# Two-layer decoder trunk: the first x transfers issued by ScalarE, the first weight tile brought in two parts

## The chip, the cores and the metric

One core of one Trainium2 chip runs the whole program. The metric is device microseconds of one execution; the median of three runs of the kernel before is 276.29 us (276.09 to 276.38).

## The reference, cut to what matters

Two layers, 256 tokens, model width 1024, everything in float32:

```python
for l in range(2):
    h = rms_norm(x, g_pre[l])
    qa, ka, va, ga, qb, kb, vb, gb, rb, qm, gm = split(h @ w_in[l])      # 1024 -> 3344
    oa = causal_attention(norm(qa), norm(ka), va) * silu(ga)             # 8 heads of 64, ALiBi
    ob = rms_norm(gated_linear_attention(qb, kb, vb, rb)) * silu(gb)     # 4 heads
    mk, mv = split(rms_norm(mem, g_mem[l]) @ w_mem_kv[l])
    om = attention(norm(qm), norm(mk), mv) * silu(gm)                    # 256 memory tokens
    x = x + concat(oa, ob, om) @ w_out[l]
```

With 256 tokens the block-sparse attention of the reference has one block, and so is plain causal attention.

## The kernel before, in words

**Products in three parts.** Every float32 operand of a large product is split into a high part, rounded to the format `fp32r`, and the low rest: `xh`, `xl` of x (times the gain `g_pre`), `whi`, `wlo` of a weight, `oh`, `ol` of the memory tokens and later of the attention outputs. A product is high by high, high by low and low by high, three TensorE matmuls (L1013 for one weight tile, L1020 for two tiles of one unit side by side). ScalarE writes a high part of a weight (L347 for the first tile, L406 for later ones) and VectorE the low part behind it (L349, L408). For x and the memory tokens the high part is ScalarE's (L260) or GpSimd's (L262) and the low part VectorE's (L302).

**The first unit.** The columns `vr` (272) and `kq` (256) of the first layer's input projection are one DRAM array `w0` of 8 tiles of 128 rows, one for each k; x lies beside it in 8 tiles k, the first with the parameters ahead of it (array `xp`). TensorE runs k = 0 to 7, at each k twelve matmuls: six of `vr` and six of `kq`. The table `LOADS` lists the transfers in the order in which `start_loads` issues them, as (x or w, first k, last k + 1, planned time of landing); all are on SyncE's queue. The reader `first_x` makes `xh` and `xl`, `first_w` makes `whi` and `wlo`, at k = 0 already in two pieces, and `first_sq` adds the squares of x for the norm (L310 on ScalarE, L315 and L318 on VectorE, called sqs). While the first data are on their way, `main` runs `WARM` matmuls on zeros (L1050).

**What sets the order.** The code is a planner: every step is a generator that asks for an engine with a cost and an earliest time, and the step that could begin first is written out next. So a change of one planned time (those of `LOADS`, `cst_ev`, the cost of the first step in `main`) moves steps on every engine, until the plans meet again. Each engine then runs its list in order. A transfer's completion is one of eight semaphores in turn, and a transfer that takes a semaphore over waits until the one before it on that semaphore has landed.

**What follows the first unit.** Weight tiles of 1 MB come through three buffers `raw`, one transfer each (L364); a tile's transfer waits for the last VectorE read of the tile before it in that buffer. The unit `ga0`, the pairs `va0 va1` and `qa0 ka0`, then the pair `mk mv` over the memory tokens follow on TensorE. The memory tokens (`memT`) are split into `oh`, `ol` and their squares summed by VectorE (L318 again); two short matmuls (L440) finish that sum. In the forget gate's chain ScalarE takes an absolute value, an exponential and, after a table load, a logarithm (L537 to L541), then VectorE makes `z` (L543) and the running sum `b` (L545).

Of the kernel before, what the change touches and what calls it, by code (L numbers as in the profile page):

```python
# [16 lines left out]
P = 128  # L17
# [11 lines left out]
PAIRK = 0  # L29
SPLIT = 7  # L30
MEMPRIO = 6
WARM = 6
FSQ = 7
STATS = 300
LOADS = (("x", 0, 1, 3100), ("w", 0, 1, 4300), ("x", 1, 2, 4600), ("w", 1, 2, 5300), ("x", 2, 4, 6000),
         ("w", 2, 3, 6700), ("w", 3, 4, 7600), ("x", 4, 6, 8300), ("w", 4, 6, 9900), ("x", 6, 8, 10600),
         ("w", 6, 8, 12100))
NB = 528
ENTER, LEAVE, CROSS = 89.0, 189.0, 60.0
SLACK, HOLD = 300.0, 900.0  # L40
# [128 lines left out]
def trunk(ctx, tc, xp_d, w0_d, memT_d, wvr_d, win_d, wmkv_d, wout_d, wup_d, cst_d, nb_d, out_d):  # L169
# [66 lines left out]
    def op(eng, cost, after=0.0, prio=None, table=None, mode="full"):  # L236
        return ("op", [(eng, cost)], after, prio, table, mode)
# [7 lines left out]
    def scost(n, psum=False, ptr=0):  # L245
        return (55 if psum else 95) + 0.83 * n + 93 * ptr
# [75 lines left out]
    def start_loads():  # L322
# [6 lines left out]
        for what, a, b, t in LOADS:  # L329
            if what == "x":  # L330
                xs = slice(L * NPRM + a * T if a else 0, L * NPRM + b * T)
                nc.sync.dma_start(xp[:, xs], xp_d[:, xs])
                plan.spawn(first_x(a, b, t), 30 - 2 * a)
            else:
                nc.sync.dma_start(raw[:, a:b], src[:, a:b])
                plan.spawn(first_w(a, b, t, raw, hi, lo, got), 29 - 2 * a)
        plan.spawn(first_sq(), 5)
        nc.sync.dma_start(cst, cst_d)
        cst_ev.set(12800)
        nc.sync.dma_start(wup, wup_d)  # L340

    def first_w(a, b, t, raw, hi, lo, got):
        for k in range(a, b):
            for n, cs in (("vr", slice(0, 272)), ("kq", slice(272, NB))) if k == 0 else (("vk", slice(0, NB)),):
                w = cs.stop - cs.start
                t1 = yield op("S", scost(w), t)
                S.activation(hi[:, k, cs], raw[:, k, cs], AF.Copy)  # L347
                t2 = yield op("V", vcost(w), t1)
                V.tensor_sub(lo[:, k, cs], raw[:, k, cs], hi[:, k, cs].bitcast(F32))  # L349
                for x in ("vr", "kq") if n == "vk" else (n,):  # L350
                    wts[0, x][k].set(t2)
        if b == KT:
            raws.release(got, t2)

# [690 lines left out]
            wrel[l, nm][k // 2].set(t)  # L1045

    def main():
        yield op("P", 4700, 0.0, None, None, "main")
        for j in range(WARM):
            TE.matmul(banks.slots[7][2][:, 0:256], lhsT=zero[:, 0:128], rhs=zero, start=True, stop=True)  # L1050
        idx = {(l, n): i for i, (l, n, _, _) in enumerate(seq)}
# [218 lines left out]
```

## Time and profile before

| what | value |
|---|---|
| median of three runs | 276.29 us (276.09 to 276.38) |
| the profiled execution's own time | 276.73 us |
| its span in the trace | 274.9 us |
| TensorE busy, matmuls | 269.3 us (98% of the span) |
| VectorE busy | 226.5 us (82%) |
| ScalarE busy | 195.2 us (71%) |
| GpSimd busy | 88.6 us (32%) |
| bytes moved | 45.76 MB, mean 166 GB/s |

The span is what the trace holds; 1.83 us of the profiled execution lie outside of it. Rows give start and duration in us. A matmul's shown duration overlaps the next one, so the pace of TensorE is read from start to start: 0.12 us for a matmul of 256 or 272 columns and 0.23 us for one of 512. Idle time in square brackets stands ahead of the row's instruction, with what ended it.

### The profile page before, as it was taken

The page shows a single profiled execution, that of the slowest core. Times are in us where ns is not written, and L with a number is a line of the kernel's source. Part 1 is how long each engine was busy: PE and PEld are TensorE (multiplying, and loading weights), DVE is VectorE, ACT ScalarE, POOL GpSimd, SP SyncE. Part 2 cuts the span into 40 slices and gives each one's busy share as a digit, 9 for nine tenths or more (in the row PEclk, how much of TensorE's full clock was granted, in tenths as well). Part 3 has the DMA queues.
Part 4 walks back from the last instruction along what each step waited for, and adds up shares of the span by engine and source line. Part 5 has one row for each costly group of instructions (what it writes and reads, how often), then busy time and mean ns, then how long its engine had stood idle before and what let it go on. Part 6 is the DMA issues. An engine that isn't in the chain of part 4 may idle for free.

```text
span 274.9 us, 5873 instructions
## 1 busy us (share of the span) xinstructions
PE 269.3 (98%) x2184; PEld 240.0 (87%) x2184; DVE 226.5 (82%) x573; ACT 195.2 (71%) x437; POOL 88.6 (32%) x107
## 2 busy tenths in 40 slices
PE   8999999999999999999999999999999999999994
PEld 7898887778998998999999887789888788999994
DVE  3998999989767998989897998989797787898621
ACT  5858995987986977957675796766986755975500
POOL 3312295650452551500062426322235520420000
PEclk9999999999999999999999999999999999999999
DMA  7999618460744142444465537048034325170111
GB/s 208 389 358 367 246 12 316 151 286 10 299 155 153 20 182 110 154 164 153 162 242 175 204 139 294 13 139 321 4 153 150 159 91 218 20 273 14 57 60 38
DMA packets 8556, 45.76 MB, mean 166 GB/s; under 512 B 960, under 2 KB 2384, under 8 KB 3536
## 3 DMA queue, kind: packets, MB, share of 16 engines
q1 hardware_dynamic: 8528, 45.39, 44.9%
q8 instruction: 17, 0.28, 0.4%
q14 instruction: 11, 0.09, 0.1%
HBM read 44.34 MB, written 1.05 MB: 165 GB/s over the span
## 4 chain that ended last, share of the span: by engine, by line
PE 86%; DVE 5%; DMA 4%; issue 1%; POOL 1%; SPq 1%; ACT 1%; POOLq 0%; DVEq 0%
PE bank L1013 48%; PE bank L1020 21%; PE bank L962 4%; PE bank L947 3%; PE bank L895 3%; DMA raw<-memT_dram 2%; PE bank L504 2%; DMA xp<-xp_dram 2%; DVE wlo L408 1%; POOL oh L262 1%; PE bank L747 1%; DVE sqs L318 1%; DVE ol L302 1%; PE bank L623 1%; PE bank L702 0%
## 5 line engine op out<-in xcount | busy, mean ns | idle before, releaser
L408 DVE TENSOR_TENSOR wlo<-raw,whi 128x512 fp32r<-128x512 f32 (+1 forms) x144 | 97.4, 699 | 13.5 <-ACT whi L406 12.1
L406 ACT ACTIVATE whi<-raw 128x512 fp32r<-128x512 f32 (+1 forms) x144 | 86.4, 625 | 20.8 <-PE bank L1013 8.9
L1013 PE MATMUL bank<-xh,whi 128*128 128x256 f32 x160 | 46.3, 289 | 0.0
L1013 PE MATMUL bank<-xl,whi 128*128 128x256 f32 x160 | 44.5, 278 | 0.0
L1013 PE MATMUL bank<-xh,wlo 128*128 128x256 f32 x160 | 44.5, 278 | 0.0
L932 POOL TENSOR_SCALAR pe<-pe,rc 128x256 f32<-128x256 f32 (+1 forms) x48 | 27.3, 583 | 39.9 <-DVE rc L929 27.0
L1013 PE MATMUL bank<-oh,whi 128*128 128x256 f32 x128 | 35.9, 280 | 0.0
L1013 PE MATMUL bank<-ol,whi 128*128 128x256 f32 x128 | 35.8, 280 | 0.0
L1013 PE MATMUL bank<-oh,wlo 128*128 128x256 f32 x128 | 35.7, 279 | 0.0
L484 POOL TENSOR_TENSOR cc<-ss,nhalf 128x8 f32<-128x8 f32 x12 | 20.9, 1746 | 42.0 <-DVE ss L482 35.2
L1020 PE MATMUL bank<-whi,xh 128*128 128x512 f32 x80 | 32.7, 409 | 0.0
L1013 PEld LDWEIGHTS bank<-xh,whi 128*128 128x128 f32 x160 | 30.1, 188 | 1.6 <-issue 1.4
L1020 PE MATMUL bank<-wlo,xh 128*128 128x512 f32 x80 | 31.4, 393 | 0.0
L1020 PE MATMUL bank<-whi,xl 128*128 128x512 f32 x80 | 31.3, 391 | 0.0
L1013 PEld LDWEIGHTS bank<-xl,whi 128*128 128x128 f32 x160 | 30.1, 188 | 0.1
L1013 PEld LDWEIGHTS bank<-xh,wlo 128*128 128x128 f32 x160 | 30.2, 189 | 0.0
L1013 PE MATMUL bank<-whi,xh 128*128 128x256 f32 (+1 forms) x96 | 28.1, 293 | 0.0
L1013 PE MATMUL bank<-wlo,xh 128*128 128x256 f32 (+1 forms) x96 | 27.6, 287 | 0.4 <-DVE wlo L349 0.3
L1013 PE MATMUL bank<-whi,xl 128*128 128x256 f32 (+1 forms) x96 | 27.1, 282 | 0.0
L1013 PEld LDWEIGHTS bank<-oh,wlo 128*128 128x128 f32 x128 | 24.3, 190 | 0.0
L1013 PEld LDWEIGHTS bank<-oh,whi 128*128 128x128 f32 x128 | 24.0, 188 | 0.2 <-issue 0.2
L1013 PEld LDWEIGHTS bank<-ol,whi 128*128 128x128 f32 x128 | 24.0, 188 | 0.1
(188 smaller groups left out, 606.0 us busy)
## 6 DMA issues: line engine op xcount, KB each, us to landing
raw<-win_dram SPq DMA_DIRECT2D x23, 1024.0 KB, 5.4
raw<-wout_dram SPq DMA_DIRECT2D x8, 1024.0 KB, 4.8
raw<-wmkv_dram SPq DMA_DIRECT2D x4, 1024.0 KB, 4.8
raw<-memT_dram SPq DMA_DIRECT2D x2, 1024.0 KB, 5.4
raw<-wvr_dram SPq DMA_DIRECT2D x1, 1088.0 KB, 5.0
raw<-w_dram SPq DMA_DIRECT2D x4, 264.0 KB, 4.5
raw<-w_dram SPq DMA_DIRECT2D x2, 528.0 KB, 7.1
nb<-nb_dram SPq DMA_DIRECT2D x1, 1024.0 KB, 8.8
```

What stands on the lines that cost most here:

```text
L262: G.tensor_scalar(dst, src, 1.0 if scale is None else scale, 1.0, op0=ALU.mult, op1=ALU.mult)
L302: V.scalar_tensor_tensor(lo[:, k], src[:, k], col(l, g0 + k), hi[:, k].bitcast(F32), op0=ALU.mult, op1=ALU.subtract)
L406: S.activation(hi[:, cs], raw[:, cs], AF.Copy)
L408: V.tensor_sub(lo[:, cs], raw[:, cs], hi[:, cs].bitcast(F32))
L484: G.tensor_tensor(c, ss, nhalf, op=ALU.pow)
L504: TE.transpose(ps[:, m, tt * P:tt * P + P], n[:, tt, m * P:m * P + P], ident)
L895: TE.matmul(bk[hh][2][:, a:b], lhsT=x[ds], rhs=y[ds], start=(j == 0), stop=(j == len(prs) - 1))
L932: G.tensor_scalar(pe[:, hh, a:b], pe[:, hh, a:b], rc[:, hh, qt:qt + 1], 1.0, op0=ALU.mult, op1=ALU.mult)
L947: TE.transpose(bk[0][2][:, dst:dst + P], pe[:, hh, src:src + P], ident)
L962: TE.matmul(po[64 * hh:64 * hh + 64, q0:T], lhsT=vv[:, j, c:c + 64], rhs=pt[:, hh, 256 * j:256 * j + T - q0], start=(j == 0), stop=(j == 1))
L1013: TE.matmul(ps, lhsT=a, rhs=b, start=(first and j == 0), stop=(lastk and j == 2))
L1020: TE.matmul(ps, lhsT=a, rhs=b, start=(first and j == 0), stop=(lastk and j == 2))
```

## The change

The table of transfers now names five kinds: the first weight tile comes as `v` (its 272 columns of `vr`) and `q` (its 256 columns of `kq`), two transfers with a semaphore each, where one transfer brought both. The transfers of x up to k = 3 (three of them: k = 0, k = 1, k = 2 and 3) are issued by ScalarE; the others of x and all of the weights stay with SyncE, which now issues `v`, `q` and three more weight tiles one behind the other. `first_w` splits what one transfer brought; the pieces at k = 0 have the widths that they had. The planned times of landing and of the first matmul are lower, and there are five matmuls on zeros instead of six.

```diff
-WARM = 6
+WARM = 5
...
-LOADS = (("x", 0, 1, 3100), ("w", 0, 1, 4300), ("x", 1, 2, 4600), ("w", 1, 2, 5300), ("x", 2, 4, 6000),
-         ("w", 2, 3, 6700), ("w", 3, 4, 7600), ("x", 4, 6, 8300), ("w", 4, 6, 9900), ("x", 6, 8, 10600),
-         ("w", 6, 8, 12100))
+LOADS = (("x", 0, 1, 2900), ("v", 0, 1, 3500), ("q", 0, 1, 4000), ("x", 1, 2, 4000), ("w", 1, 2, 5100), ("x", 2, 4, 5600),
+         ("w", 2, 3, 6300), ("w", 3, 4, 7300), ("x", 4, 6, 7600), ("w", 4, 6, 9500), ("x", 6, 8, 9700),
+         ("w", 6, 8, 11800))
...
-                nc.sync.dma_start(xp[:, xs], xp_d[:, xs])
+                (nc.scalar if b <= 4 else nc.sync).dma_start(xp[:, xs], xp_d[:, xs])
...
-                nc.sync.dma_start(raw[:, a:b], src[:, a:b])
-                plan.spawn(first_w(a, b, t, raw, hi, lo, got), 29 - 2 * a)
+                cs = {"v": slice(0, 272), "q": slice(272, NB), "w": slice(0, NB)}[what]
+                nc.sync.dma_start(raw[:, a:b, cs], src[:, a:b, cs])
+                plan.spawn(first_w(a, b, t, cs, raw, hi, lo, got), 29 - 2 * a)
...
-        cst_ev.set(12800)
+        cst_ev.set(12400)
...
-        yield op("P", 4700, 0.0, None, None, "main")
+        yield op("P", 4100, 0.0, None, None, "main")
```

Lines of the kernel after stand two further down from L349 on: its L1015, L1022 and L442 are L1013, L1020 and L440 of the kernel before.

**ScalarE, start of the program.** Before (`xh` is the high part of an x tile, `whi` of a weight; 272 and 256 columns are the two pieces at k = 0, 528 is a whole tile):

```order
L323 ACT_TABLE_LOAD
L323 ACTIVATE warm<-ones 128x1
L260 ACTIVATE xh<-xp 128x256
L347 ACTIVATE whi<-raw 128x272
L260 ACTIVATE xh<-xp 128x256
L347 ACTIVATE whi<-raw 128x256
L347 ACTIVATE whi<-raw 128x528
```

Now:

```order
L323 ACT_TABLE_LOAD
L323 ACTIVATE warm<-ones 128x1
L332 DMA xp<-xp_dram 128x302
L332 DMA xp<-xp_dram 128x256
L332 DMA xp<-xp_dram 128x512
L260 ACTIVATE xh<-xp 128x256
L347 ACTIVATE whi<-raw 128x272
L347 ACTIVATE whi<-raw 128x256
L347 ACTIVATE whi<-raw 128x528
```

Three issues of transfers stand behind the table load and the first activation, and the x tile of k = 1 has gone from ScalarE to GpSimd.

**VectorE, first unit.** Before (`xl`, `wlo` are the low parts, `sqs` the sum of squares of x; two equal rows are written once with x2):

```order
L349 TENSOR_TENSOR wlo<-raw,whi 128x528
L315 TENSOR_TENSOR sqs_129<-sq_103 128x256
L302 SCALAR_TENSOR_TENSOR xl<-xp,xh 128x256 x2
L349 TENSOR_TENSOR wlo<-raw,whi 128x528 x2
L318 TENSOR_TENSOR sqs_129<-sqs_129,sq_104 128x256
L302 SCALAR_TENSOR_TENSOR xl<-xp,xh 128x256 x2
L318 TENSOR_TENSOR sqs_129<-sqs_129,sq_104 128x256
L349 TENSOR_TENSOR wlo<-raw,whi 128x528
L318 TENSOR_TENSOR sqs_129<-sqs_129,sq_103 128x256
L302 SCALAR_TENSOR_TENSOR xl<-xp,xh 128x256
L349 TENSOR_TENSOR wlo<-raw,whi 128x528
```

Now:

```order
L349 TENSOR_TENSOR wlo<-raw,whi 128x528
L302 SCALAR_TENSOR_TENSOR xl<-xp,xh 128x256 x2
L315 TENSOR_TENSOR sqs_129<-sq_103 128x256
L349 TENSOR_TENSOR wlo<-raw,whi 128x528 x2
L302 SCALAR_TENSOR_TENSOR xl<-xp,xh 128x256 x2
L318 TENSOR_TENSOR sqs_129<-sqs_129,sq_104 128x256 x2
L349 TENSOR_TENSOR wlo<-raw,whi 128x528
L302 SCALAR_TENSOR_TENSOR xl<-xp,xh 128x256
L349 TENSOR_TENSOR wlo<-raw,whi 128x528
```

The first `wlo` row is k = 1, the pair is k = 2 and 3, then come k = 4 and k = 5. The first sum now stands behind the two `xl` of k = 2 and 3, and the sum that stood between `wlo` of k = 4 and of k = 5 has gone behind them.

**TensorE, after the sum over the memory tokens.** Before (`zl` and `ee` belong to the linear attention; `whi,xh` is the pair `qa0 ka0`, `whi,oh` the pair `mk mv`):

```order
L689 MATMUL bank_95<-zl_135,ee 64x128
L1020 MATMUL bank_98<-whi,xh 128x512
L1020 MATMUL bank_98<-wlo,xh 128x512
L1020 MATMUL bank_98<-whi,xl 128x512
L1020 MATMUL bank_99<-whi,xh 128x512
L1020 MATMUL bank_99<-wlo,xh 128x512
L1020 MATMUL bank_99<-whi,xl 128x512
L702 MATMUL bank_94<-qbd,kf 32x64
```

Now:

```order
L691 MATMUL bank_95<-zl_135,ee 64x128
L1022 MATMUL bank_99<-whi,xh 128x512
L1022 MATMUL bank_99<-wlo,xh 128x512
L1022 MATMUL bank_99<-whi,xl 128x512
L1022 MATMUL bank_92<-whi,oh 128x512
L1022 MATMUL bank_92<-wlo,oh 128x512
L1022 MATMUL bank_92<-whi,ol 128x512
L704 MATMUL bank_94<-qbd,kf 32x64
```

Three matmuls of the pair `qa0 ka0` have gone from here to ahead of L440, and the first three of `mk mv` have come forward from behind L702 and L623. Two more moves are told without rows. ScalarE makes the first `oh` tile of the memory tokens itself, which was GpSimd's. On VectorE the last `wlo` of `va1`, whose buffer the transfer of the memory tokens waits for, stood ahead of `z` and `b` and now stands behind them. After about the first third of the program every engine runs the same list before and after.

## Rows read from the trace of the kernel before

**Rows 1.** Page: the chain that ended last, shares by engine.
```profile
PE 86%; DVE 5%; DMA 4%; issue 1%; POOL 1%; SPq 1%; ACT 1%; POOLq 0%; DVEq 0%
```

**Rows 2.** Timeline: start us, us, engine, line, operation, output and input, count [idle].
```profile
1.17 4.60 PE L1050 MATMUL bank<-ob 128*128 128x256 f32 x12 [1.17 <-DVE ones L1180]
...
4.96 0.19 PEld L1050 LDWEIGHTS bank<-ob 128*128 128x128 f32 x1
...
5.39 0.19 PEld L1013 LDWEIGHTS bank<-whi,xh 128*128 128x128 f32 x1
```

**Rows 3.** Timeline, to 12 us: the first issue, ScalarE reads that waited.
```profile
0.72 0.37 SPq L332 DMA_DIRECT2D xp<-xp_dram  x1
...
2.99 0.51 ACT L260 ACTIVATE xh<-xp 128x256 fp32r<-128x256 f32 x1 [0.78 <-DMA xp<-xp_dram]
...
4.00 0.43 ACT L347 ACTIVATE whi<-raw 128x272 fp32r<-128x272 f32 x1 [0.50 <-DMA raw<-w_dram]
...
6.04 0.65 ACT L347 ACTIVATE whi<-raw 128x528 fp32r<-128x528 f32 x1 [0.40 <-DMA raw<-w_dram]
...
11.18 0.64 ACT L347 ACTIVATE whi<-raw 128x528 fp32r<-128x528 f32 x1 [0.77 <-DMA raw<-w_dram]
```

**Rows 4.** Chain of work in order of time: start us, us, what.
```profile
2.56 4.76 DMA xp<-xp_dram
...
28.57 5.97 DMA raw<-memT_dram
...
34.69 2.97 POOL oh L262
...
244.70 26.71 PE bank L1013 x225
```

**Rows 5.** Timeline, PEld waits in the first unit; their sum (us, times, longest).
```profile
7.48 0.19 PEld L1013 LDWEIGHTS bank<-wlo,xh 128*128 128x128 f32 x1 [0.34 <-DVE wlo L349]
...
9.46 0.19 PEld L1013 LDWEIGHTS bank<-wlo,xh 128*128 128x128 f32 x1 [0.47 <-DVE wlo L349]
...
PEld bank L1013 <- DVE wlo L349: 1.2, 4, 0.5
```

**Rows 6.** Timeline, VectorE in the first unit.
```profile
8.70 1.43 DVE L349 TENSOR_TENSOR wlo<-raw,whi 128x528 fp32r<-128x528 f32 x2
...
12.48 0.42 DVE L318 TENSOR_TENSOR sqs<-sqs,sq 128x256 f32<-128x256 f32 x1
...
13.19 0.48 DVE L302 SCALAR_TENSOR_TENSOR xl<-xp,xh 128x256 fp32r<-128x256 f32 x1 [0.30 <-POOL xh L262]
...
13.60 0.70 DVE L349 TENSOR_TENSOR wlo<-raw,whi 128x528 fp32r<-128x528 f32 x1
```

**Rows 7.** Stretches: us, busy PE PEld DVE ACT POOL, PEclk, DMA share, GB/s.
```profile
2.00:3.00 1.00, 1.00 (x3) 0.77 (x3) 0.00 (x0) 0.21 (x2) 0.83 (x6) 1.00 0.96 279
...
10.00:12.00 2.00, 2.00 (x18) 2.00 (x18) 1.88 (x6) 1.24 (x3) 0.85 (x2) 1.00 1.03 401
```

**Rows 8.** Timeline, 45 to 51 us: memory sums, and a memory weight.
```profile
45.26 0.39 PE L1020 MATMUL bank<-whi,xl 128*128 128x512 f32 x1
...
45.52 0.41 DVE L318 TENSOR_TENSOR sqs<-sqs,sq 128x256 f32<-128x256 f32 x1
...
45.99 0.61 PE L440 MATMUL bank<-ones,sqs 128*128 128x1 f32 x4 [0.34 <-DVE sqs L318]
...
50.33 0.68 DVE L408 TENSOR_TENSOR wlo<-raw,whi 128x512 fp32r<-128x512 f32 x1
```

**Rows 9.** Timeline, ScalarE before its first transfer's data.
```profile
0.71 1.28 ACT L323 ACT_TABLE_LOAD   x1 [0.71 <-PEq L1257]
...
2.01 0.20 ACT L323 ACTIVATE warm<-ones 128x1 f32<-128x1 f32 x1
```

**Rows 10.** Timeline, VectorE around the memory transfer.
```profile
29.02 0.59 DVE L543 SCALAR_TENSOR_TENSOR z<-z,az 128x256 f32<-128x256 f32 x1 [0.48 <-ACT az L541]
...
37.69 0.69 DVE L302 SCALAR_TENSOR_TENSOR ol<-raw,xp,oh 128x256 fp32r<-128x256 f32 x1 [0.38 <-POOL oh L262]
```

More of the change, by code (lines that the diff above doesn't have):

```diff
@@ L331, in start_loads, with first_w @@
                 xs = slice(L * NPRM + a * T if a else 0, L * NPRM + b * T)
-                nc.sync.dma_start(xp[:, xs], xp_d[:, xs])
+                (nc.scalar if b <= 4 else nc.sync).dma_start(xp[:, xs], xp_d[:, xs])
                 plan.spawn(first_x(a, b, t), 30 - 2 * a)
             else:
-                nc.sync.dma_start(raw[:, a:b], src[:, a:b])
-                plan.spawn(first_w(a, b, t, raw, hi, lo, got), 29 - 2 * a)
+                cs = {"v": slice(0, 272), "q": slice(272, NB), "w": slice(0, NB)}[what]
+                nc.sync.dma_start(raw[:, a:b, cs], src[:, a:b, cs])
+                plan.spawn(first_w(a, b, t, cs, raw, hi, lo, got), 29 - 2 * a)
         plan.spawn(first_sq(), 5)
         nc.sync.dma_start(cst, cst_d)
-        cst_ev.set(12800)
+        cst_ev.set(12400)
         nc.sync.dma_start(wup, wup_d)
-    def first_w(a, b, t, raw, hi, lo, got):
+    def first_w(a, b, t, cs, raw, hi, lo, got):
+        w = cs.stop - cs.start
         for k in range(a, b):
[L344 to L351, printed above, removed]
+            t1 = yield op("S", scost(w), t)
+            S.activation(hi[:, k, cs], raw[:, k, cs], AF.Copy)
+            t2 = yield op("V", vcost(w), t1)
+            V.tensor_sub(lo[:, k, cs], raw[:, k, cs], hi[:, k, cs].bitcast(F32))
+            if cs.start == 0:
+                wts[0, "vr"][k].set(t2)
+            if cs.stop == NB:
+                wts[0, "kq"][k].set(t2)
         if b == KT:
```

## The prediction

> **What bounds the kernel now.** I read the chain of work that ended last first: TensorE holds 86% of it, and its last piece is one unbroken run of matmuls [rows 1, 4]. Next to it, the timeline by engine shows where TensorE does not run at its own pace. From the first matmul on zeros to the end there are few such places: four waits of weight loads in the first unit, 1.2 us together, the longest at k = 2 (0.47) and k = 1 (0.34) [rows 5]; and one later: the matmul ahead of L440 starts at 45.26, is through its 512 columns at 45.26 + 0.23 = 45.49, and L440 starts at 45.99, because VectorE's sum ran from 45.52 to 45.93 [rows 8]. That is a hole of 0.50 us. After it I find none to the end of the trace. So the end moves by what TensorE's work moves by, and the change is worth what it takes from or adds to the 1.2 us, the 0.50 us and the start. VectorE is the engine behind the first unit: 1.88 of the 2.00 us from 10 to 12 [rows 7].
>
> The profiled execution took 276.73 us, 1.83 of it outside the span of 274.9, and lies 0.44 above the median of 276.29. I sum against 276.73 and take the difference over to the median.
>
> **The change part by part.**
>
> **One pass of zeros fewer.** The last load of a zero tile begins at 4.96, the first real one at 5.39 [rows 2]: the last pass (two loads, 0.21 apart) is 0.43 us, while the twelve matmuls of zeros took 4.60 [rows 2], 0.38 each on the mean. So a pass taken from the end lets the first product come 0.43 us sooner if its data are there; were it one of the slower ones, up to 0.77. By the rows they are: x of k = 0 is split from 2.99 to 3.50 and `whi` of `vr` from 4.00 to 4.43 [rows 3], its `wlo` ends near 4.9. The planned cost of the first step (4700 to 4100) is the planner's alone. The granted clock stands at 1.00, 2.4 GHz, from 2 to 3 us already [rows 7], and TensorE is as busy with real products as with zeros, so I price no loss of clock. At k = 0 this is 0.43 us gained. But k = 1 waits 0.34 us now: its weight lands at 6.04, ScalarE takes 0.65 for it, VectorE about 0.7, and the weight load follows at 7.48 [rows 3, 5, 6]. If the landing stays, these steps stay, and the 0.43 us turn into a wait of 0.34 + 0.43 there. Net: 0 as long as the weight of k = 1 lands where it did; 0.43 at the other end.
>
> **Two transfers for the first tile, x on another queue.** This removes no byte. From 2 to 3 us the DMA engines are already busy 0.96 of the time, at 279 GB/s, and from 10 to 12 us 1.03 (records overlap) at 401 [rows 7]. So what is issued sooner must share engines that are already full: I take the landings of k = 1 and later as unmoved, 0, and the later ones surely so (the last tiles, read at 11.18 after a wait of 0.77 [rows 3], have all bytes of the unit ahead of them). The gain end: were the first microseconds to run at 401 instead of 279, the tile of k = 1, with 0.15 + 0.27 + 0.13 MB of x and weights ahead of its own 0.27, would land some 0.5 to 0.9 us sooner. The loss end is in the rivals. SyncE loses three issues (one is 0.37 us [rows 3]) and gains one; its later issues come earlier, but stand in the queue behind what is not yet moved.
>
> **VectorE's order in the first unit.** The first sum stood ahead of the `xl` of k = 2 and 3, in time in which VectorE would have waited for x of k = 2 (landed 2.56 + 4.76 = 7.32 [rows 4]). Now it stands behind them, right ahead of `wlo` of k = 2. A sum shows 0.42, and two neighbours overlap by some 0.07 (`xl` starts at 13.19, shows 0.48, and the next starts at 13.60) [rows 6]: 0.35. `wlo` of k = 2 began at 8.70 [rows 6] and goes to 9.05; TensorE, which began that load at 9.46 after 0.47 of waiting [rows 5], to 9.81: +0.35 there. It is made up for later. Ahead of `wlo` of k = 5 stood a sum of 0.42 and 0.30 of waiting for GpSimd's `xh`, before it began at 13.60 [rows 6]. Now the sum stands behind it, and ScalarE makes the `xh` of k = 6 ahead of `whi` of k = 5, so that the `xl` ahead of `wlo` need not wait for GpSimd: some 0.6 us of VectorE are free where TensorE waited. The two other waits of the four, 1.2 - 0.47 - 0.34 = 0.4 us [rows 5], lie at k = 4 and 5; the 0.35 lost at k = 2 takes the place of the one, and the rest goes. The unit ends, at k = 7, by my count 0.15 us earlier: **-0.15** (ends: +0.35, if k = 2 is not caught up, and -0.43, if the pass of zeros comes through whole).
>
> **L440.** Three matmuls of `qa0 ka0` that stood behind L440 and those after it now stand ahead of it: 3 x 0.23 = 0.69 us of work. TensorE comes to L440 at 45.49 - 0.15 + 0.69 = 46.03; the sums end at 45.93 [rows 8] if VectorE keeps its time. The hole of 0.50 closes: **-0.50**. The cover is thin, 0.10 us; a VectorE that is 0.6 us later opens it again.
>
> **The first three of `mk mv`.** They go from behind L702 and L623 to right there, some 2.3 us sooner, and need the high and low parts of the memory weights and `ol`. `wlo` of the first quarter of `mv` began at 50.33 and ends at 51.01 [rows 8], and would now be wanted at 49.9 to 50. VectorE's order is moved along with it, so part of it is made up; bounds 0 and 0.9, nearer to the hole of 0.50 that one late operand of VectorE makes in rows 8 than to 0.9: **+0.30**.
>
> **ScalarE takes the first `oh`; `va1`'s last `wlo` behind `z` and `b`.** GpSimd's `oh` took 2.97 us and the memory chain waited on it [rows 4]; ScalarE's x tile took 0.51 [rows 3]. That frees some 2.4 us in a chain which VectorE closes (`ol` at 37.69 after 0.38 of waiting for it [rows 10]). Against it the memory transfer, issued at 28.57 and landed at 34.54 [rows 4], now waits for a `wlo` that stands behind `z` and `b`. `z` began at 29.02 after 0.48 us of waiting for ScalarE's logarithm and took 0.59 [rows 10]; with as much for `b`, an estimate, and 0.68 for the `wlo` [rows 8] the issue comes at 29.02 + 0.59 + 0.59 + 0.68 = 30.9 and the landing at 36.9. Before, `oh` was there at 34.69 + 2.97 = 37.66; now it is at 36.9 + 0.51 = 37.4. The one hides the other, with 0.25 to spare: **0**, from a landing of 37.2 on a loss.
>
> **Sum**: -0.15 - 0.50 + 0.30 = -0.35; 276.73 - 0.35 = 276.38 as this execution, 276.29 - 0.35 = 275.94, **275.9 us**, as the median. A measurement of this kernel can tell about 0.2%, 0.55 us, from no change; by that the forecast itself is "no change, if anything faster".
>
> **The rivals.**
>
> *The two queues share evenly (no change).* With one queue the transfers go in the order of need. With two, x of k = 2 and 3 (0.26 MB) runs at the same time as the weight of k = 1, and both land when both are moved. In the trace x of k = 2 and 3 landed at 2.56 + 4.76 = 7.32 [rows 4] and the weight at 6.04; moved together the weight comes near 7.3. Then `whi` to 7.95, `wlo` to 8.65: k = 1 starts 1.2 us late less what the shorter waits at k = 2 and 5 give back, the unit ends +0.5, L440 closes (-0.50), `mk mv` 0 to +0.3: 276.3 to 276.6, say **276.4**. For it: nothing in the rows orders two queues. Against it: all issues stood on one queue, so no row shows two. The Trainium skill (DMA: Bandwidth & Descriptors, Queues, rings and completion order) states that each DMA engine goes round its queues in turn; no row of this trace shows it, since before only one queue moves the data; by that rule this rival is the course of the first 8 us. It leaves the sum's later terms alone.
>
> *The x transfers wait for ScalarE (slower).* In the program they stand behind the table load (0.71 to 1.99) and an activation that ends at 2.21 [rows 9]; SyncE issued x at 0.72 [rows 3]. If the issue waits for the end of these, x of k = 0 lands about 2 us later, near 5.0 instead of 2.97. After it come 0.51 for `xh` and 0.48 for `xl`; TensorE wants them, one pass of zeros earlier, from 5.0 on, so it loses from a landing of some 4.25 on. The first unit then ends up to +0.85, and with L440 closed the whole is +0.35 to +0.85: **276.9**. Against it: the table load waited for TensorE's sequencer for 0.71 us [rows 9], so ScalarE's issue need not stand where its work does. The Trainium skill (Perfetto Trace Analysis, DVE / Act Engine Instruction) describes a queue in which an instruction waits for its engine while the sequencer goes on; by that the issues would go out near 0.8, and no row here shows a transfer issued by ScalarE.
>
> *Two queues together are quicker (faster).* If 279 GB/s [rows 7] is what one queue gives at the start and two give up to the 401 of later, k = 1 lands 0.5 to 0.9 sooner; then the 0.43 us of zeros and part of the 1.2 us of waits go as far as VectorE (1.88 of 2.00 busy [rows 7]) lets them: -0.9 to -1.0, **275.4**. Against it: engines 0.96 busy at 279 GB/s.
>
> *The memory tokens come late (slower).* If the transfer shares its engines with weights and lands past 37.2, `ol` and the sums are late by as much; a delay of 0.55 us, less L440's cover of 0.10, gives a hole of 0.45 again in place of the -0.50: -0.15 + 0.45 + 0.30 = +0.60, **276.9**. Against it: behind the memory chain VectorE has other work, and the other tiles' `oh` start sooner than they did when GpSimd was busy for 2.97 us with the first [rows 4].
>
> **How the numbers follow.** Forecast 0.36 (of it faster 0.11, the same 0.23, slower 0.02); even share 0.20 (same 0.15, slower 0.05); x waits for ScalarE 0.16 (slower 0.10, same 0.06); quicker 0.16 (all faster); memory late 0.12 (slower 0.08, same 0.04). Together faster 0.27, same 0.48, slower 0.25. The range takes the quicker case with 0.3 of spread below it, 275.1, and the slower ones' price, 276.9; past both lie the ends that I give 0.2 together.
>
> **What would show it.** First unit: the read of k = 1's weight by ScalarE (6.04 before): earlier says quicker, near 7.3 even share. The first x read (2.99): near 5.0 says that ScalarE held its issues. The first real weight load at about 4.96 says that the zeros were the limit; a wait at k = 1 of 0.77 that they were swallowed. Wait at L440: none, and the sums before 46.0. Weight loads of `mk mv`: 0.3 us of waiting. Memory landing before 37. I am wrong in the argument, not in a size, if TensorE shows new holes past the first third, or if the end does not move with TensorE's start of the second unit.

## The result, and the profile after

The changed kernel takes 280.8 us (median of three, 279.69 to 281.33) where the kernel before took 276.29: 4.5 us more, and outside the range of 275.1 to 276.9. The ratio on record is 1.0148, 95% interval 1.0128 to 1.0169, which is 4.1 us. The profiled execution is the 280.8 one, 4.1 us over the profiled 276.73 of before; its span is 279.0 us against 274.9.

The page of the kernel after, busy tenths and granted clock in 40 slices of 7 us:

```profile
PE   8899997998999999999999999999999999999995
...
PEclk9999999799999999999999999999999999999998
```

Before, every slice of the clock was 9, and TensorE's first slice was its only one under 9 but the last. Now TensorE's row has weak slices at the start, a 7 at 42 to 49 us and an 8 at 63 to 70, and the clock's row a 7 right behind the first of these, at 49 to 56. Behind that the two traces run side by side. The first of these rows is of the kernel before, the second of the kernel after:

```profile
73.19 0.60 PE L504 MATMUL bank<-cst,nh 128*128 128x128 f32 x4
...
77.38 0.60 PE L506 MATMUL bank<-cst,nh 128*128 128x128 f32 x4
```

The same matmuls come 4.19 us later, and the span ends 4.1 later. So all of the loss arises in the first 77 us, where the lists differ.

The waits of TensorE's weight loads in the kernel after (engine and line, what it waited for: us, times, longest), to be read against [rows 5] and [rows 8]:

```profile
PEld bank L442 <- DVE sqs L318: 2.1, 1, 2.1
...
PEld bank L1015 <- DVE wlo L349: 1.8, 4, 0.6
PEld bank L1015 <- DVE kl L802: 1.3, 1, 1.3
```

The hole at the memory sums (L440 before, L442 now) was to close; it is the largest of the trace. The wait for `kl` is new. TensorE's timeline around the sums, in the kernel after:

```profile
46.37 0.39 PE L1022 MATMUL bank<-whi,xl 128*128 128x512 f32 x1
48.44 0.61 PE L442 MATMUL bank<-ones,sqs 128*128 128x1 f32 x4 [1.68 <-DVE sqs L318]
48.91 0.78 PE L1022 MATMUL bank<-whi,xh 128*128 128x512 f32 x1
...
51.74 0.97 PE L687 MATMUL bank<-zl,ee 64*128 64x256 f32 x4
```

and behind the sums in the kernel before:

```profile
46.46 0.48 PE L1020 MATMUL bank<-whi,xh 128*128 128x512 f32 x1
...
48.02 0.70 PE L685 MATMUL bank<-zl,ee 64*128 64x256 f32 x4
```

TensorE is through at 46.37 + 0.23 = 46.60 and starts the sums' matmuls at 48.44: 1.84 us where [rows 8] have 0.50. The six matmuls after it take 48.91 to 51.74, 2.83 us, where the same six took 1.56 before (46.46 to 48.02). The stretches of the kernel after go with it (us, busy PE PEld DVE ACT POOL, PEclk, DMA share, GB/s):

```profile
46.00:48.00 2.00, 0.76 (x4) 0.29 (x2) 2.00 (x8) 2.00 (x6) 0.44 (x1) 1.00 0.05 21
48.00:50.00 2.00, 1.56 (x7) 1.37 (x8) 2.00 (x6) 2.00 (x5) 0.00 (x0) 0.73 0.03 4
50.00:52.00 2.00, 2.00 (x7) 1.16 (x7) 2.00 (x8) 0.71 (x3) 0.71 (x1) 0.50 0.75 303
```

TensorE was idle for most of 46 to 48, and behind that the granted clock is 0.50, 1.2 GHz. The loss is added up from instructions that stand in both traces: the first pair of the second unit +0.43 (26.67 against 26.24); L442 +2.45, less 0.69 for the three matmuls that now stand ahead of it, so 1.33 more; the six matmuls +1.27; the short ones behind them +0.26; some 0.3 is regained by 68 us; the hole ahead of `qm` (the unit behind `mk mv`, of 256 columns) +1.1. Together 4.1.

### The profile page after: what moved, and what is told of

It reads as the page before. It is cut to its first block, busy times and chain, and to the rows that moved or that the text cites. A ratio compares the mean times of both kernels' runs of the same rounds, so it can differ in the third digit from the quotient of the medians.

```text
span 279.0 us, 5871 instructions
## 1 busy us (share of the span) xinstructions
PE 270.6 (97%) x2182; PEld 240.5 (86%) x2182; DVE 226.7 (81%) x573; ACT 194.0 (70%) x435; POOL 85.0 (30%) x109
## 4 chain that ended last, share of the span: by engine, by line
PE 77%; DVE 9%; DMA 4%; issue 4%; POOL 3%; ACT 1%; ACTq 0%; DVEq 0%; POOLq 0%
PE bank L1015 44%; PE bank L1022 17%; PE bank L964 4%; PE bank L949 3%; PE bank L897 3%; DVE wlo L410 3%; DMA raw<-win_dram 2%; DMA xp<-xp_dram 2%; POOL zl L262 2%; PE bank L506 2%; PE bank L749 1%; POOL qbd L562 1%; DVE sqs L318 1%; ACT whi L408 1%; DVE ol L302 1%
## 5 line engine op out<-in xcount | busy, mean ns | idle before, releaser
L1015 PE MATMUL bank<-xh,whi 128*128 128x256 f32 x160 | 46.3, 289 | 0.0
L1015 PE MATMUL bank<-xl,whi 128*128 128x256 f32 x160 | 44.5, 278 | 0.0
L1015 PE MATMUL bank<-xh,wlo 128*128 128x256 f32 x160 | 44.5, 278 | 0.0
L486 POOL TENSOR_TENSOR cc<-ss,nhalf 128x8 f32<-128x8 f32 x12 | 21.9, 1832 | 47.6 <-DVE ss L484 41.3
L1015 PE MATMUL bank<-oh,whi 128*128 128x256 f32 x128 | 35.9, 280 | 0.0
L1015 PE MATMUL bank<-ol,whi 128*128 128x256 f32 x128 | 35.8, 279 | 0.0
L1015 PE MATMUL bank<-oh,wlo 128*128 128x256 f32 x128 | 35.7, 279 | 0.0
L1022 PE MATMUL bank<-whi,xh 128*128 128x512 f32 x80 | 33.3, 416 | 0.0
L1022 PE MATMUL bank<-wlo,xh 128*128 128x512 f32 x80 | 31.9, 398 | 0.0
L1022 PE MATMUL bank<-whi,xl 128*128 128x512 f32 x80 | 31.8, 397 | 0.0
L1015 PEld LDWEIGHTS bank<-xh,whi 128*128 128x128 f32 x160 | 30.1, 188 | 1.6 <-issue 1.4
L1015 PEld LDWEIGHTS bank<-xl,whi 128*128 128x128 f32 x160 | 30.1, 188 | 0.1
L1015 PEld LDWEIGHTS bank<-xh,wlo 128*128 128x128 f32 x160 | 30.2, 189 | 0.0
L1015 PE MATMUL bank<-whi,xh 128*128 128x256 f32 (+1 forms) x96 | 28.4, 296 | 0.9 <-DVE kl L802 0.9
L1015 PE MATMUL bank<-wlo,xh 128*128 128x256 f32 (+1 forms) x96 | 27.5, 287 | 0.9 <-DVE wlo L349 0.9
L1015 PE MATMUL bank<-whi,xl 128*128 128x256 f32 (+1 forms) x96 | 27.1, 282 | 0.0
L1015 PEld LDWEIGHTS bank<-oh,wlo 128*128 128x128 f32 x128 | 24.3, 190 | 0.0
L1015 PEld LDWEIGHTS bank<-oh,whi 128*128 128x128 f32 x128 | 24.0, 188 | 0.2 <-issue 0.2
L1015 PEld LDWEIGHTS bank<-ol,whi 128*128 128x128 f32 x128 | 24.0, 188 | 0.1
```

The costliest lines, as they stand in the source:

```text
L486: G.tensor_tensor(c, ss, nhalf, op=ALU.pow)
L1015: TE.matmul(ps, lhsT=a, rhs=b, start=(first and j == 0), stop=(lastk and j == 2))
L1022: TE.matmul(ps, lhsT=a, rhs=b, start=(first and j == 0), stop=(lastk and j == 2))
```

## The experiments

Ratios are to the kernel before on the same chip, with 95% intervals; times are medians.

### Planned times or transfers

The change does two things: it moves transfers, and it gives the planner other times, from which it writes other lists. One kernel has the transfers alone, with the old times:

```diff
-LOADS = (("x", 0, 1, 2900), ("v", 0, 1, 3500), ("q", 0, 1, 4000), ("x", 1, 2, 4000), ("w", 1, 2, 5100), ...
+LOADS = (("x", 0, 1, 3100), ("v", 0, 1, 4300), ("q", 0, 1, 4300), ("x", 1, 2, 4600), ("w", 1, 2, 5300), ...
...
-        cst_ev.set(12400)
+        cst_ev.set(12800)
...
-        yield op("P", 4100, 0.0, None, None, "main")
+        yield op("P", 4700, 0.0, None, None, "main")
```

> The transfers of the changed kernel (x on ScalarE's queue, the first tile in two parts, five matmuls on zeros) with the planned times of before, so that from the second unit on every engine runs the list of before. Theory 'order': the 4.5 us come from the lists that the new planned times made; then only the first unit's own loss is left (TensorE's first pair began at 26.67 instead of 26.24) and part of it goes into the hole of 0.50 at L440: 276.0 to 276.9, no new hole after 18 us. Rival 'transfers': the late x is what makes the memory sums late; then the hole of about 2 us at that stage comes back and the time is 279 or more.

The other has the new times, and so the new lists, with the transfers of before:

```diff
-WARM = 5
+WARM = 6
...
-                (nc.scalar if b <= 4 else nc.sync).dma_start(xp[:, xs], xp_d[:, xs])
+                nc.sync.dma_start(xp[:, xs], xp_d[:, xs])
...
-                nc.sync.dma_start(raw[:, a:b, cs], src[:, a:b, cs])
+                what == "q" or nc.sync.dma_start(raw[:, a:b], src[:, a:b])
```

> The planned times of the changed kernel, so the same lists on TensorE, VectorE, ScalarE and GpSimd from the first row on, with the transfers of before (all on SyncE's queue, the first tile in one, x between the weights) and six matmuls on zeros. Theory 'order': the hole of 2.1 us at the memory sums and the one of 1.3 us before kl come back, 279.5 to 281. Rival 'transfers': 276.0 to 277.0 and no hole over 0.8 us.

Measured: transfers alone 277.01 us, 1.0018 (1.0004 to 1.0031); lists alone 279.7 us, 1.0120 (1.0094 to 1.0146). In the first, TensorE's hole at L442 is 0.51 us (46.36 after a matmul that began at 45.62), as before. In the second it is back, 1.85 us (48.53 after a matmul that began at 46.45), and behind it the granted clock falls again:

```profile
50.00:52.00 2.00, 2.00 (x7) 0.96 (x6) 2.00 (x9) 1.32 (x4) 0.71 (x1) 0.50 0.83 311
```

"Order" holds: most of the loss is in the lists (0.0120 of the ratio), some 0.5 us in the transfers (0.0018).

### GpSimd's list, or GpSimd's pace

VectorE, in the kernel after, waits for `oh`, which is GpSimd's (timeline of GpSimd, then of VectorE):

```profile
36.30 4.58 POOL L262 TENSOR_SCALAR zl<-wz,cst 128x256 f32<-128x256 f32 x2 [6.65 <-DVE wz L668]
40.85 0.48 POOL L262 TENSOR_SCALAR oh<-raw,xp 128x256 fp32r<-128x256 f32 x1
```

```profile
38.87 1.28 DVE L410 TENSOR_TENSOR wlo<-raw,whi 128x512 fp32r<-128x512 f32 x2
41.37 0.69 DVE L302 SCALAR_TENSOR_TENSOR ol<-raw,xp,oh 128x256 fp32r<-128x256 f32 x1 [1.22 <-POOL oh L262]
```

Two copies `zl` of the linear attention stand ahead of `oh` and take 4.58 us, the first of them 4.13; the same shape takes 0.48 right behind. The first test puts GpSimd's `oh` ahead of them again, and leaves all other lists:

```diff
+            f = lambda: G.tensor_scalar(dst, src, ...)
+            nz[0] += tag == "zl"
+            if tag == "zl" and nz[0] <= 3:
+                held.append(f)
+            else:
+                f()
+                if tag == "oh" and held:
+                    held.pop(0)()
```

> The changed kernel, but GpSimd's copies zl are written behind its oh tiles (oh, zl, oh, zl, oh, zl, then the other oh) as in the kernel before; every other engine's list stays. Theory 'GpSimd': the two zl (4.58 us from 36.30 on) are what the memory tiles wait for; then GpSimd's first oh starts when the memory tokens land, near 35.6 instead of 40.85, the sums end by 46.5 and the hole at the sums is under 0.5: 276.3 to 277.8. Rival 'late transfer': the memory transfer, issued at 30.79 instead of 28.57, is what counts; then the hole stays over 1 us and the time over 279.

Measured: 280.38 us, 1.0149 (1.0123 to 1.0175); the hole at the sums is 1.6 us. My "GpSimd's list" fell. But the rival, the late transfer, did not win either, as GpSimd's row of this run shows:

```profile
37.85 4.62 POOL L264 TENSOR_SCALAR oh<-raw,xp 128x256 fp32r<-128x256 f32 x1 [6.16 <-DMA raw<-memT_dram]
42.45 0.48 POOL L264 TENSOR_SCALAR zl<-wz,cst 128x256 f32<-128x256 f32 x1
```

The memory tokens were there at 37.8, and the one `oh` took 4.62 us, until VectorE came to its next `ol` and had to wait for it (0.30 us, to 42.51). In the kernel after, too, the first `zl` ended near the start of VectorE's wait (40.43, the wait began at 40.15). (The run's first unit was 2 us late as well; see "The rest, and the spread".) So a new theory: GpSimd is starved while VectorE works without pauses. In the kernel before, VectorE's wait of 0.38 us for GpSimd's first `oh` [rows 10] would be that pause, and the change took it away by giving that `oh` to ScalarE. Two kernels bear on it: GpSimd makes the first `oh` again, with its list of before (`held` as in the edit above),

```diff
+        if eng == "S" and tag == "oh" and not noh[0]:
+            noh[0] = 1
+            G.tensor_scalar(dst, src, scale, 1.0, op0=ALU.mult, op1=ALU.mult)
+            if held:
+                held.pop(0)()
```

> The changed kernel with GpSimd's list of before for the memory tokens: it makes the first oh too, and its zl copies stand between the oh tiles; the other lists stay, ScalarE's without that one oh. New theory 'starved GpSimd': a GpSimd instruction that meets a VectorE without pauses goes on until VectorE pauses (2.97 us before, 4.58 for two in the changed kernel, 4.62 for the first oh in the run with oh ahead of zl, against 0.48 for the same shape elsewhere); with the first ol waiting for GpSimd again, VectorE pauses near 38, the oh is done near 38.2 and the next ones follow 0.9 apart: the two waits of VectorE for oh (1.22 and 0.30) shrink to under 0.6 together, and the hole at the sums from 2.1 to 1.0 to 1.4, the rest being VectorE's longer list (five or six small el and wz, about 1.1 us, ahead of the last sums). Time 0.8 to 2 us under the changed kernel. Rival 'late transfer': the hole stays at 1.8 to 2.2 and the time within 0.5 of the changed kernel.

or makes none of the eight, which all go to ScalarE:

```diff
-        if eng == "S":
+        if eng == "S" or tag == "oh":
```

> The changed kernel with all eight oh tiles of the first layer's memory tokens on ScalarE, which sat idle from 41.9 to 44.9; GpSimd keeps its zl copies only. 'Starved GpSimd': VectorE no longer waits for an oh (1.52 us of waits go), the sums end near 46.9 instead of 48.4 and the hole is 0.4 to 0.8; the clock does not fall behind it; 277.0 to 279.0, at least 1.5 us under the changed kernel. 'Late transfer': the sums end within 0.4 us of where they did, hole over 1.6. If VectorE's list alone made the hole, it is 1.2 to 2.

Measured: 279.95 us, 1.0134 (1.0105 to 1.0164) with the first `oh` on GpSimd, and 278.76 us, 1.0084 (1.0057 to 1.0111) with all on ScalarE. GpSimd's first rows in the one and in the other:

```profile
35.55 2.49 POOL L260 TENSOR_SCALAR oh<-raw,xp 128x256 fp32r<-128x256 f32 x1 [6.04 <-DMA raw<-memT_dram]
38.02 0.47 POOL L269 TENSOR_SCALAR zl<-wz,cst 128x256 f32<-128x256 f32 x1
```

```profile
36.41 5.28 POOL L262 TENSOR_SCALAR zl<-wz,cst 128x256 f32<-128x256 f32 x3 [6.65 <-DVE wz L668]
```

In the first, with its first `ol` waiting for GpSimd, VectorE paused at 37.7, and the `oh` was done at 38.0, as the theory has it; the waits of VectorE for `oh` came down from 1.52 to 0.69 us (0.39 and 0.30), and the hole from 1.84 to 1.54 us. That is less than I expected (1.0 to 1.4), and by the timed runs it is not shown to be faster: its interval covers 1.0148. With all `oh` on ScalarE, VectorE waits for none, the hole is 0.28 us (46.72 to 47.00), the clock stays at 1.00, and the ratio falls by 0.0064, some 1.8 us. So VectorE's waits for GpSimd's `oh` make most of the hole, as the kernel with all `oh` on ScalarE shows.

The other part is VectorE's list. From the first `ol` (37.69 before, 37.73 after) to the last sum (45.52 and 47.97) it takes 2.4 us longer: 1.52 are the two waits for `oh`, and some 1.0 is five small steps (`el`, `wz`) that have come ahead of the last sum, less one that has left. TensorE itself comes 1.1 us later (0.43 + 0.69), so the small steps alone would have been covered, as the hole of 0.28 with all `oh` on ScalarE shows.

"Until VectorE pauses" did not hold as a rule. With all `oh` on ScalarE, GpSimd's first `zl` took 3.52 us, to 39.93, and the next two 0.91 and 0.89, while VectorE worked without a pause from 36 to 42 (stretch of that run); and in the kernel before, GpSimd made four `oh` in 3.91 us next to a VectorE that was busy all the time (its row, then a stretch):

```profile
36.00:42.00 6.00, 6.00 (x28) 4.93 (x27) 6.00 (x16) 6.00 (x14) 5.28 (x3) 1.00 0.18 48
...
39.56 3.91 POOL L262 TENSOR_SCALAR oh<-raw,xp 128x256 fp32r<-128x256 f32 x4
...
39.00:44.00 5.00, 5.00 (x24) 4.09 (x23) 5.00 (x12) 4.00 (x10) 4.47 (x5) 1.00 0.60 192
```

So a GpSimd copy next to a busy VectorE took anything from 0.48 to 4.62 us. What sets it is open: four of the slow ones ended next to a pause of VectorE, that of 3.52 did not; with the lists of before a first `oh` took 0.58 beside a VectorE without a pause (33.53, one pass of zeros fewer); and no run measured the two engines alone.

The Trainium skill (SBUF — State Buffer, Who interferes with whom) says that VectorE and GpSimd contend for one pair of ports under an exclusive lock, and that a VectorE operation with two SBUF inputs, which `wlo` and `ol` are, contends with a GpSimd operation that reads SBUF. The rows agree that both can lose: a GpSimd copy took 0.48 us beside a VectorE that waited and up to 4.62 us beside a busy one, and VectorE's `ol`, 0.47 us where GpSimd stood still (43.66 and 45.86 before), took 0.69 where GpSimd's `zl` ran beside it (41.37 in the kernel after).

### What the hole costs beside its length

```diff
+        if Rout is None:
+            for j in range(4):
+                TE.matmul(ps[:, 256:512], lhsT=ob[:, 0, 0:128], rhs=ob[:, 0], start=True, stop=True)
```

> The changed kernel with four matmuls on a tile that nobody needs (256 columns, about 1.7 us together) ahead of the memory sums' matmuls, inside the hole of 2.1 us, so that TensorE is busy in it; they are work left over and change no output. Theory 'clock': the six matmuls after the hole, which took 2.8 us at half the granted clock, take 1.4 to 1.6 again and the clock stays at 1.0 from 48 to 54; 1.2 to 1.7 us less than the changed kernel, 279.1 to 279.6 where that stands at 280.8, and the spread between its runs (279.7 to 281.3) gets smaller. Rival: the hole alone costs the time, the clock in the rows means nothing for the end: within 0.4 us of the changed kernel.

Measured: 279.9 us, 1.0129 (1.0107 to 1.0150). TensorE's timeline:

```profile
46.47 1.89 PE L443 MATMUL bank<-ob 128*128 128x256 f32 x8
48.32 0.61 PE L445 MATMUL bank<-ones,sqs 128*128 128x1 f32 x4
48.78 0.48 PE L1025 MATMUL bank<-whi,xh 128*128 128x512 f32 x1
...
50.35 0.70 PE L690 MATMUL bank<-zl,ee 64*128 64x256 f32 x4
```

The six matmuls take 48.78 to 50.35, 1.57 us instead of 2.83, and the span is 277.6 instead of 279.0: in the traces the clock is worth 1.3 to 1.4 us. The ratios differ by 0.0019, some 0.5 us, and their intervals overlap, so by the timed runs the size is not settled. The clock does not fall in every run: of the changed kernel's three timed runs two have a mean granted clock of 0.991 and 0.993 (280.8 and 281.33 us) and one of 0.999 (279.69). Nor did it fall behind every hole: behind those of 1.84 us (changed kernel) and 1.85 (lists alone) it stood at 0.50, behind those of 1.60 (`oh` ahead of `zl`) and 1.54 (first `oh` on GpSimd) it stayed at 1.00, as the stretches of the latter two show:

```profile
50.00:52.00 2.00, 1.75 (x10) 1.50 (x10) 2.00 (x5) 2.00 (x5) 0.00 (x0) 1.00 0.23 33
...
48.00:50.00 2.00, 1.98 (x10) 1.50 (x10) 2.00 (x4) 2.00 (x5) 0.00 (x0) 1.00 0.28 45
```

### The second hole

On top of all `oh` on ScalarE, `kl` goes ahead of three `att` copies and two `wlo` on VectorE:

```diff
+        elif tag == "acc":
+            late.append(lambda: V.tensor_copy(dst, src))
...
-            V.tensor_sub(lo[:, cs], raw[:, cs], hi[:, cs].bitcast(F32))
+            f = lambda cs=cs: V.tensor_sub(lo[:, cs], raw[:, cs], hi[:, cs].bitcast(F32))
+            late.append(f) if l == 0 and nm in ("qm", "qa1") and a == 4 else f()
...
             V.tensor_sub(lo, src, hi.bitcast(F32))
+            while late:
+                late.pop(0)()
```

> The run with all oh on ScalarE (278.76, ratio 1.0084) with one more edit: on VectorE kl, the last reader of the PSUM bank that the unit qm gets next, goes ahead of the three att copies and the two wlo that stood in front of it. Theory 'bank': TensorE's hole of 1.4 us ahead of qm is the wait for that bank; kl starts as soon as ScalarE's kh is there (65.4 instead of 66.7), TensorE comes at 66.4, the hole is under 0.3, and 1.0 to 1.4 us of it reach the end: 277.3 to 277.9. Rival: the copies and wlo that go behind kl are waited for just as long (wlo of qm's third quarter by qm itself, att by the matmuls on vb); the hole comes back as waits of that size within 5 us, and the time stays within 0.4 of the other run.

and then one `att` copy goes from VectorE to ScalarE:

```diff
-        if eng == "S" or tag == "oh":
+        if eng == "S" or tag in ("oh", "rect"):
```

> As the run with kl ahead, and the second of the two first att copies of the linear attention (128x256, out of PSUM) is ScalarE's again, as it was in the kernel before, and not VectorE's, where it stood behind three wlo. Theory: TensorE's wait of 0.9 us ahead of L704 shrinks to the 0.4 that the kernel before had there; 0.3 to 0.6 under the run with kl ahead, 276.8 to 277.5, which leaves the first unit's loss of about 0.5 and little else of the 4.5 us. Rival: another late VectorE operand takes its place there (the memory units' wlo), no gain.

Measured: 278.75 us, 1.0074 (1.0053 to 1.0096), and 278.56 us, 1.0067 (1.0038 to 1.0097). The hole itself went as expected: TensorE in the kernel after, and VectorE with `kl` ahead,

```profile
68.12 0.40 PE L1022 MATMUL bank<-whi,ol 128*128 128x512 f32 x1
69.42 0.39 PE L1015 MATMUL bank<-whi,xh 128*128 128x256 f32 x1 [0.90 <-DVE kl L802]
```

```profile
65.53 0.69 DVE L805 TENSOR_TENSOR kl<-bank,kh 128x512 fp32r<-128x512 f32 x1 [0.45 <-ACT kh L258]
66.14 0.87 DVE L264 COPY att<-acc 32x256 f32<-32x256 f32 x3
```

and with `kl` ahead TensorE's last matmul of the `oh` and `ol` kind begins at 66.27 and the first of `qm` at 66.50, 0.23 later, its usual pace; no wait for `kl` is left. In the new plan `qm` writes into PSUM bank 95, whose last reader is `kl`; in the old one it had bank 96, free earlier. That was in the lists, as a name in each row, and I had compared the rows without it. But the ratios moved by 0.001 and 0.0007, some 0.3 and 0.2 us and far inside their intervals, where I expected 1.0 to 1.4 and 0.3 to 0.6 us. The trace with `kl` ahead shows where the first of these went. Seven us further on TensorE has two waits that the run without this edit does not have:

```profile
73.38 0.19 PEld L766 LDWEIGHTS bank<-qsh,blk 128*128 128x128 f32 x1 [0.38 <-ACT qsh L258]
73.84 0.19 PEld L767 LDWEIGHTS bank<-qsl,blk 128*128 128x128 f32 x1 [0.27 <-DVE qsl L764]
```

From the first matmul of `qm` to the matmuls on `nh` it takes 8.63 us (66.50 to 75.13) and not 7.97 (67.46 to 75.43), so about 0.4 of the 1.1 us is left. That is the rival's course, with other operands than the ones it named. The runs of the last kernel spread from 277.19 to 280.5 us, which led to the next test.

### The rest, and the spread

```diff
-WARM = 5
+WARM = 6
...
-                (nc.scalar if b <= 4 else nc.sync).dma_start(xp[:, xs], xp_d[:, xs])
+                nc.sync.dma_start(xp[:, xs], xp_d[:, xs])
...
+                what == "q" or nc.sync.dma_start(raw[:, a:b], src[:, a:b])
```

> As the run with oh on ScalarE, kl ahead and att on ScalarE (278.56, from 277.19 to 280.5), but with the transfers of before and six matmuls on zeros: what is left of the new planned times is the order of the other steps. Theory 'landing': what that run still loses, and its spread of 3 us, is x of k = 2 and 3 on ScalarE's queue, which was read anywhere from 7.34 to 8.57 in the profiles, while the new list of ScalarE holds the weights of k = 2 and 3 behind it; with x between the weights on one queue it is read at 7.3 to 7.4, the time is 276.4 to 277.2 and the spread under 2 us. Rival: the rest of the lists costs it; then the time stays at 277.8 to 278.8.

Measured: 277.36 us, 1.0030 (1.0020 to 1.0040), from 276.86 to 277.76: 1.2 us less by the medians, 1.0 by the ratios, whose intervals just overlap, and a spread of 0.9 instead of 3.3 us. The time came out just over my range (276.4 to 277.2), and the edit takes back three things at once, so which of them did it is not shown. x of k = 2 is read at 6.78 (at 7.32 with the same transfers in the run of the lists alone), where seven profiles with the new lists and x on ScalarE's queue have it at 7.59 to 8.57. The latest of these, the run with `oh` ahead of `zl`, shows what that does (ScalarE's timeline, then stretches):

```profile
8.57 0.51 ACT L262 ACTIVATE xh<-xp 128x256 fp32r<-128x256 f32 x1 [2.75 <-DMA xp<-xp_dram]
```

```profile
8.00:10.00 2.00, 0.84 (x8) 0.64 (x6) 0.88 (x3) 1.43 (x3) 0.48 (x1) 1.00 0.98 350
...
12.00:14.00 2.00, 2.00 (x12) 2.00 (x11) 1.97 (x5) 2.00 (x5) 0.76 (x1) 0.53 0.88 310
14.00:16.00 2.00, 2.00 (x13) 2.00 (x12) 2.00 (x6) 1.17 (x3) 0.00 (x0) 0.62 0.87 291
```

The weights of k = 2 and 3 stand behind that read on ScalarE, TensorE runs dry at 8 to 10, the clock falls to about half, and the second unit's first pair comes at 28.71. In the other six of these profiles it comes at 26.53 to 26.91. So a late x can cost 2 us; that it makes the spread of the timed runs is likely but not shown, as one execution of each kernel is profiled. In the last kernel's own trace the pair comes at 25.87, before 26.24, and the stretch from `qm` to `nh` still takes 8.62 us where the kernel before had 7.85 (65.34 to 73.19): that is about the 0.8 us that are left of 1.0030.

### The start

In the kernel before, one matmul on zeros fewer:

```diff
-WARM = 6
+WARM = 5
```

> The kernel before with five matmuls on zeros instead of six, nothing else. 'Swallowed' (as predicted): the first product comes 0.43 us sooner, the wait at k = 1 grows by as much, the first pair of the second unit stays at 26.2: within 0.2 us of the kernel before. Rival: it comes through, 0.3 to 0.45 us faster; or the granted clock falls and it is slower.

And in the kernel with the transfers alone, the first x back on SyncE:

```diff
-                (nc.scalar if b <= 4 else nc.sync).dma_start(xp[:, xs], xp_d[:, xs])
+                (nc.scalar if 1 < b <= 4 else nc.sync).dma_start(xp[:, xs], xp_d[:, xs])
```

> As the run with the transfers of the changed kernel and the old planned times, but x of k = 0 is again the first issue on SyncE; x of k = 1 and of k = 2, 3 stay on ScalarE's queue. Theory 'late issue': the first x came late (read at 3.90 instead of 2.99) because ScalarE issues it at 1.18, behind an activation that waits for VectorE's ones, and behind more weights; now it is read at 2.9 to 3.1, the first product starts at 5.0 to 5.2, and the second unit's first pair at 26.0 to 26.3: 0 to 0.3 us faster than the kernel before, 0.3 to 0.7 under that run. Rival 'shared queues': it is x of k = 2, 3, read at 7.7 instead of 7.3, that sets the end of the unit; then the pair stays at 26.5 to 26.7 and the time 0.2 to 0.6 over the kernel before.

Measured: one pass of zeros fewer, 276.6 us, 1.0003 (0.9986 to 1.0019), the first pair at 26.28: swallowed. The first x back on SyncE, 276.89 us, 1.0012 (0.9994 to 1.0030), pair at 26.43: x of k = 0 is read at 3.02, as the theory had it, but the second half of the first weight tile is read at 5.95 instead of 5.24, and the pair comes 0.17 earlier than with the transfers alone (26.60), short of the 26.0 to 26.3 that I expected. The intervals of this run and of the transfers alone overlap; that it is faster is not shown.

### A version from it

The edit that sends all eight `oh` to ScalarE, in the kernel before:

```diff
-        if eng == "S":
+        if eng == "S" or tag == "oh":
```

> The kernel before with all eight oh tiles of the first layer's memory tokens on ScalarE; nothing else. If GpSimd's pace is what VectorE waited for (0.38 at the first ol), the sums end 0.3 to 0.6 sooner than 45.93 and the hole of 0.50 at L440 shrinks to 0 to 0.2: 0.2 to 0.5 us faster than the kernel before, ratio 0.998 to 0.9995. Rival: ScalarE, which makes the memory units' whi from 45.05 on, gets late with its other tiles (va, zl) and TensorE waits for those instead: no gain, or up to 0.5 slower.

Measured over 12 runs: 276.14 us, 0.9987 (0.9970 to 1.0004). The hole at L440 is 0.17 us (after a matmul that began at 44.98), and the span is 274.0 us against 274.9, of which 0.28 stand in the first unit, which the edit does not touch:

```profile
45.38 0.61 PE L440 MATMUL bank<-ones,sqs 128*128 128x1 f32 x4
```

It has the lowest ratio of the kernels here, but the interval reaches just past no change: that it is faster than the kernel before is not shown.

## Why the prediction was wrong

**What bounds the kernel**: right. TensorE stood still at no place after the first third, and the end moved by 4.1 us as TensorE did by 77 us (4.19).

**One pass of zeros**: right; swallowed, ratio 1.0003. (The row at 4.96 is the first load of the last pass, not the last load, which begins at 5.17; the 0.43 stands.)

**Landings unmoved**: wrong. x of k = 0 was read at 4.22, not 2.99 [rows 3]. ScalarE's first issue is at 1.18 (the page's name for its sequencer is ACTq):

```profile
1.18 0.86 ACTq L332 DMA_DIRECT2D xp<-xp_dram  x2
...
4.22 0.51 ACT L260 ACTIVATE xh<-xp 128x256 fp32r<-128x256 f32 x1 [2.01 <-DMA xp<-xp_dram]
```

My rival "x waits for ScalarE" had the right place but the wrong point: the issue did not wait for the activation to end at 2.21. It came right behind the end of VectorE's write of `ones` at 1.13, which the activation ahead of it reads; that it waited for that is not tested alone. My argument against the rival, from the Trainium skill's queue in which an instruction waits while the sequencer goes on (Perfetto Trace Analysis, DVE / Act Engine Instruction), had the issue near 0.8; the trace does not bear that out here. The premise of "quicker" came true in part: from 2 to 3 us the rate fell from 279 to 206 GB/s, then from 3 to 5 us it rose from 266 and 240 to 328 and 364. But the bytes that came sooner were not the ones waited for: the weight of k = 1 was read at 6.49, not 6.04. The first unit ended +0.43, where I had -0.15.

**VectorE's order in the first unit**: half right. The wait at k = 5 is gone; at k = 2 the load is at 10.14, not 9.81, as x of k = 2 was read at 7.71, not 7.34.

**L440**: this step failed, in its condition "if VectorE keeps its time". The sums ended at 48.4 instead of 45.93, the hole became 1.84 instead of 0, and -0.50 became +1.33. Of VectorE's delay 1.52 us are waits for `oh` and some 1.0 the small steps that had come ahead of the last sum, a moved list that I had not costed.

**ScalarE takes the first `oh`, priced 0**: here the failure begins. The memory transfer was issued as worked out (30.79, forecast 30.9) but landed 4.8 us later, at 35.6, and not at 36.9. That ScalarE's `oh` began at 36.92 is luck: ScalarE was not waiting for the transfer, it had other work ahead of it (kernel after).

```profile
30.79 0.33 SPq L366 DMA_DIRECT2D raw<-memT_dram x1
...
36.18 0.83 ACT L589 ACTIVATE el<-el 128x768 f32<-128x768 f32 x1
36.92 0.49 ACT L260 ACTIVATE oh<-raw,xp 128x256 fp32r<-128x256 f32 x1
```

I then took GpSimd to be 2.4 us freer, and the other `oh` to start sooner. This is the step that fell. GpSimd's list had changed with it (two `zl` ahead), and its 2.97 us went with the place and not with the `oh`: whatever it had first there took 2.49 to 4.62 us in the runs with the new lists, and VectorE's waits for `oh` grew from 0.38 to 1.52 us. The rival "memory late" named the right place and the wrong cause, and its price, one hole of 0.45, lacked the clock behind it.

**The clock**: not in the sum at all. I priced it for the zeros only. In the profiled run a hole of 1.84 us was followed by 1.27 us more for six matmuls.

**The bank of `qm`**: not in the sum; +1.1 us in the trace. With the wait removed about 0.4 us of it was left in the trace, and the ratio moved by less than its interval, so what it costs in the timed median is not settled.

**The first three of `mk mv`, +0.30**: no such wait; the six matmuls from 53.02 to 54.60 run at their pace.

**The range**: its upper end was the price of one rival at a time. Here the late x and the late sums came together, and with them two costs that no rival had, the clock and the bank.

## What to carry to other kernels

A planner's input is the whole program: where a change of a few planned times rewrites every list, cost each moved list, with the buffer and bank names in it, before counting a gain of tenths. A slow step's duration need not be its own: here, with the new lists, the copy that stood first on GpSimd was the slow one, whichever it was, so taking one away freed nothing. And a hole in a saturated TensorE can cost twice, its length and the slower matmuls behind it: that was so behind the holes of 1.84 and 1.85 us and not behind those of 1.54 and 1.60.

## What the runs showed of the hardware that I had not expected

A GpSimd copy of 128x256 that reads SBUF took 0.48 us next to a VectorE that waits, and between 0.48 and 4.62 us next to one that works. Those of 2.49, 2.97, 4.13 and 4.62 us ended within 0.4 us of the start of VectorE's next pause; one of 3.52 us ended in the midst of VectorE's work. Two transfer queues at the start moved 328 to 364 GB/s from 3 to 5 us where one moved 240 to 266, and x of k = 2 was read at 7.59 to 8.57 in kernels with the same first issues, 1 us apart.
